# SyncE's issue order written out for the first two attention stages of a hybrid decoder block

## The chip, the cores and the metric

The kernel runs on one core of one Trainium2 chip. The core has five engines with a queue each: TensorE (PE) for matmuls, VectorE (DVE), ScalarE (ACT) and GpSimd (POOL) for everything else, and SyncE (SP), which in this kernel issues every DMA. An engine takes its instructions strictly in the order of its queue; an instruction that waits for a semaphore holds up all that stand behind it. A DMA's data is moved by 16 shared DMA engines after SP has issued it.

The metric is the time of one execution on the device, in microseconds (us). Before the change three runs took 628.25, 628.37 and 627.59 us; the median is 628.25 us.

## The reference: what is computed

One layer of a decoder block over 528 positions (16 learned meta tokens ahead of 512 tokens), width 1024, all in float32:

```
u    = RMSNorm(h)
proj = u @ w_in                # cq, ckv, k_pe, z_mla, fq, fk, fv, f_logit, z_fox, gate_a, gate_b
MLA:  q = RMSNorm(cq) @ w_uq   # 16 heads: 64 plain + 32 rotary columns
      k, v = RMSNorm(ckv) @ w_ukv;  k also has the shared rotary k_pe
      o_mla = causal softmax(q k^T / sqrt(96)) v
FoX:  cum = cumsum(log_sigmoid(f_logit + b))
      o_fox = causal softmax(fq fk^T / 8 + cum[t] - cum[s]) fv
y_mla = (o_mla * silu(z_mla)) @ w_br_mla;   y_fox = (o_fox * silu(z_fox)) @ w_br_fox
out   = h + RMSNorm((sig(gate_a) * y_mla + sig(gate_b) * y_fox) @ w_out)
```

## The kernel before

**Tiling.** Activations stay on the core, transposed, as a high and a low part (`uTh`, `uTl`). Each weight block of 128 columns is loaded by SP into one of three buffers `wraw` (line 133), cut by ACT into a high part `wh` (line 142) and by POOL, or DVE, into the rest `wl` (line 118), and multiplied in three passes. One such block with its matmuls and its ending is a `unit`; a unit's `make` cuts its weights and asks for the loads of the next three units (`nxt`).

**Stages.** Attention runs in 16 stages: for each of eight pairs of heads first the FoX branch (stages 0, 2, 4, ...), then the MLA branch (1, 3, 5, ...). A stage has, on PE, scores of the first three query blocks (`s0`), scores of the fourth (`s1`), and then the `fill`: the projections that the next stage needs. The values of a stage (`va`, tile `ov`) are computed in the stage after it, between that stage's `s0` and `s1`. Between scores and values lie the softmax (DVE takes the row bound `nb`; ACT the exponentials `sf`, line 693), the normalised probabilities `pn` in two float16 parts (ACT line 721, DVE line 722, meta columns by POOL lines 708 to 713), and their transposition into `pts` by DMA (line 729): for query blocks 0 to 3 two transfers each, of 3, 5, 7 and 9 tiles. `n0` issues the six of the first three blocks, `n1` the two of the fourth.

**Columns and rotary parts.** FoX scores add the cumulated gate by a fourth matmul with `CT`, whose two rows per head come from `c_dram` (line 280) when the pair's `fk` projection is done. MLA scores add the rotary part with `QP`, read from `qpe_dram` (line 507). The rotary projections are made in two halves (`pe_unit`): pairs 0 to 3 before stage 0, pairs 4 to 7 in stage 1's fill. Each half ends in `turn` (POOL, line 560), `rest` (ACT line 563, POOL line 118 on tile `gT`) and four writes of 256 KB to `qpe_dram` (line 566).

**Accumulators.** The projections of a fill share three PSUM accumulators (`acc`), the scores four banks (`stp`); a bank is free again when the engine that reads it is done.

**What sets the order.** PE's order is the written one in all of attention. In stage 0 POOL, ACT and DVE are in written order too. Everything else, SP's queue in all attention stages included, is placed by a scheduler that orders ready instructions by priorities and its own cost estimates.

In the trace's terms, `fq`, `fk`, `v`, `z`, `mq`, `mk` and `ppe` are units, `hlq` and `hlk` their results in two parts, `vT`, `vt`, `vm`, `vp` the steps of the values' operand, and `sil` the gated `z`.

Of the kernel before, what the change touches and what calls it, by code (L numbers as in the profile page):

```python
# [49 lines left out]
def f32(ap):  # L50
    return ap.bitcast(F32)
# [3 lines left out]
def block_kernel(ctx: ExitStack, tc: tile.TileContext, x, meta_tokens, pre_norm_g, w_in, fox_forget_b,  # L55
                 mla_q_norm_g, mla_kv_norm_g, w_uq, w_ukv, w_br_mla, w_br_fox, w_out, post_norm_g,
                 rope_tok, rope_pe, out):
    nc = tc.nc
# [32 lines left out]
    def mm(*a, **k):  # L91
        nc.tensor.matmul(*a, **k)  # L92
# [96 lines left out]
    def acc(name):  # L189
        return accp.tile([128, 512], F32, tag="acc", name=name)  # L190
# [3 lines left out]
    def unit(name, getw, act, nk, sls, done):  # L194

        st = {}
        out = []

        def make(*a):
            if "w" not in st:  # L200
                st["w"] = getw(*a)
                for load in getattr(out[0][1], "nxt", ()):
                    load()

        for i, sl in enumerate(sls):
            n = sl.stop - sl.start
            for k in range(nk):
                def fn(i=i, sl=sl, k=k, n=n):
                    make()
                    if k == 0:  # L210
                        st["ps"] = acc(f"{name}{i}")
                    ps = st["ps"][:, :n]
                    (wh, wl), (ah, al) = st["w"], act(k)
                    for q, (w, a) in enumerate(((wh, ah), (wh, al), (wl, ah))):
                        mm(ps, w(k), a[:, sl], start=(k == 0 and q == 0), stop=(k == nk - 1 and q == 2))
                    if k == nk - 1:
                        done(i, ps)
                out.append((3 * n / 2.4, fn))
        out[0][1].make = make
        if hasattr(getw, "load"):  # L220
            out[0][1].load = getw.load
        return out
# [16 lines left out]
    def run(steps):  # L239
        for _, fn in steps:  # L240
            fn()
# [227 lines left out]
    E_ = mybir.EngineType  # L469
    with ExitStack() as att:  # L470
# [35 lines left out]
        def load_qp(pr):  # L506
            nc.sync.dma_start(f32(QP), qpe_dram[2 * pr : 2 * pr + 2].rearrange("h i x f s -> (h i x f) s"))
# [123 lines left out]
        def z_unit(br, pr):  # L631
            def done(i, pz):
                sil = aw.tile([128, S], F32, tag="sil", name=f"sil{br}{pr}")
                with tc.high_priority(offset=60):
                    nc.scalar.activation(sil, pz, AF.Tanh, scale=0.5)
                    nc.vector.scalar_tensor_tensor(out=sil, in0=sil, scalar=1.0, in1=pz, op0=ALU.add, op1=ALU.mult)
                sils[br, pr] = sil
            return unit(f"z{br}{pr}", win_w((O_ZM, O_ZF)[br], pr), u_act, KD, REAL, done)

        def attention(br, pr):  # L640
# [4 lines left out]
            q, k = hls["q", br, pr], hls["k", br, pr]  # L645
# [11 lines left out]
            def sf_of(h, b):  # L657
                o, n = SF_STEP * (b % 3), 144 + 128 * b
                return sfs[b // 3][:, h, o : o + n]
# [38 lines left out]
            def norm(g):  # L698
                def fn(mid=int):
                    b0, nb_ = GRP[g][0], len(GRP[g])  # L700
                    su, ri = (sums[t][:, :, b0 : b0 + nb_] for t in ("su", "ri"))
                    nc.vector.tensor_scalar(out=su, in0=su, scalar1=1.0 / PSCALE, scalar2=None, op0=ALU.mult)
                    nc.vector.reciprocal(ri, su)  # L703

                    mt = aw.tile([128, 2, nb_, META], F32, tag=f"mt{g}", name=f"mt{nm_}{g}", bufs=1)
                    src = sfs[g][:, :, 0 : SF_STEP * nb_].rearrange("p h (b c) -> p h b c", b=nb_)[:, :, :, 0:META]
                    dst = pn[g][:, :, 0 : PN_STEP * nb_].rearrange("p h (b t) c -> p h b t c", b=nb_)[:, :, :, 0]
                    nc.gpsimd.tensor_tensor(out=mt, in0=src, in1=ri.unsqueeze(3).broadcast_to([128, 2, nb_, META]),  # L708
                                            op=ALU.mult)
                    hi, lo, hi2 = (dst[:, :, :, 32 * i : 32 * i + META] for i in range(3))  # L710
                    nc.gpsimd.tensor_copy(hi, mt)
                    nc.gpsimd.tensor_tensor(out=lo, in0=mt, in1=hi, op=ALU.subtract)
                    nc.gpsimd.tensor_copy(hi2, mt)
                    for b in GRP[g]:
                        for h in range(2):
                            sf = sf_of(h, b)[:, META:].rearrange("p (j c) -> p j c", c=128)
                            t0 = PN_STEP * (b % 3) + 1
                            hi, lo = (pn[g][:, h, t0 : t0 + 2 * b + 2].rearrange("p (j l) c -> p j l c", l=2)[:, :, i]
                                      for i in range(2))
                            rib = sums["ri"][:, h, b : b + 1]  # L720
                            nc.scalar.activation(hi, sf, AF.Copy, scale=rib)  # L721
                            nc.vector.scalar_tensor_tensor(out=lo, in0=sf, scalar=rib, in1=hi, op0=ALU.mult,  # L722
                                                           op1=ALU.subtract)
                    for b in GRP[g]:
                        if b == 1:
                            mid()
                        for h in range(2):
                            t0 = PN_STEP * (b % 3)
                            nc.sync.dma_start_transpose(
                                out=pts[h][:, 0 : 2 * b + 3, 128 * b : 128 * b + 128],  # L730
                                in_=pn[g][:, h, t0 : t0 + 2 * b + 3].rearrange("p t c -> p (t c)"))
                return fn
# [23 lines left out]
        def feed(br, pr):  # L756

            q = (q_mla, q_fox)[br](pr)
            k = (k_mla, k_fox)[br](pr)
            v, vts[br, pr] = v_unit(br, pr)  # L760
            return q, k, v
# [10 lines left out]
        for si, (br, pr) in enumerate(stages):  # L772
            last = si + 1 == len(stages)
            if not last:
                q, k, v = feed(*stages[si + 1])
            if br == 1:

                za, zb = z_unit(1, pr), z_unit(0, pr)
                fill = za + vts[br, pr] + q + zb[:4] + k + zb[4:6] + v + zb[6:]
            elif not last:  # L780
                fill = q[:3] + vts[br, pr] + q[3:] + k + v
            else:
# [5 lines left out]
                fill = g[:4] + vts[br, pr] + g[4:] + g2[:4] + [(100, g_scale)] + g2[4:]  # L788
            if si == 0:
                early = za[0][1], q[0][1], zb[0][1]  # L790
                rope0 = pe_turn, pe_rest
# [9 lines left out]
        late = []  # L801
        for si, (br, pr) in enumerate(stages):
            (s0, e0), (s1, e1), n0, n1, va = attention(br, pr)

            fill = fills[si]
            with ExitStack() as head:
                if si == 0:
                    head.enter_context(tc.manual_schedule(engines={E_.PE, E_.Pool, E_.Activation, E_.DVE}))
                    za, q, zb = early
                    turn, rest = rope0  # L810
                    za.make()
                    q.make()
                    lo = []
                    turn()
                    s0()
                    zb.make(nc.vector, lo)
                    e0({(0, 1): lambda: rest(1), (1, 1): lambda: rest(0)})
                    s1()
                    n0(lambda: load_qp(0))
                    lo[0]()  # L820
                    e1()
                    run(fill[:4])
                else:
                    s0()
                    e0()
                    for fn in late:
                        fn()
                    s1()
                    e1()
                    run(fill[:4])  # L830
                    n0()
            run(fill[4:11])
            n1()
            run(fill[11:])
            late = [va]
        run(tail[:4])
        mgates[0].make()
# [13 lines left out]
    with ExitStack() as mg:  # L851
# [42 lines left out]
        class Acts(Cuts):  # L894
            late = "BD"
# [26 lines left out]
        class Weights(Cuts):  # L922
            late = "BC"
# [4 lines left out]
            def load(self):  # L928
                p = self.p
                self.raw = raw = rwp.tile([128, 2, KD, 128], F32, tag="yraw", name=f"yraw{p}")  # L930
                for f in range(2):
                    c = 256 * p + 128 * f
                    nc.sync.dma_start(raw[:, f], wbr[1][:, :, c : c + 128])
                columns(self, f"1{p}")
                super().__init__(f"aop{p}", aop, 128, [raw[:, f] for f in range(2)], self.c[0])
# [69 lines left out]
        def make():  # L1005
            if todo:
                todo.pop(0).make()
            if todo:
                todo[0].load()
# [106 lines left out]
    with rctx, ExitStack() as og:  # L1116
# [29 lines left out]
        for c in range(4):  # L1146
            w = pre[c] if c < len(pre) else wout_unit(0, c)
# [68 lines left out]
```

## Time and profile before

| | |
|---|---|
| median of three runs | 628.25 us |
| profiled execution | 627.48 us, of which span from first to last instruction 625.1 us |
| mean granted TensorE clock | 0.992 |
| busy: PE, ACT, DVE, POOL | 601.1 (96%), 384.7, 380.8, 188.9 us |
| chain of waits, by engine | PE 92%, DVE 2%, ACT 2%, DMA 2%, SP's sequencer 1% |
| time that PE waited for transposed probabilities (`pt`) | 5.2 us, twice |

How to read it: a row of the timeline has the start in us from the span's start, the duration, the engine and line, the operation with its tiles and the count, and in brackets the idle time of that engine just before and what ended it. SPq is SP's sequencer; its rows are DMA issues, and a long one means that the issue itself took long. A row with a count covers several instructions of one kind. The granted clock is a share of full speed. All of attention lies between 71 and 414 us; stage 0 begins at 71.1, stage 1 at 89.97, stage 2 at 124.47 and stage 3 at 144.28 us.

### The profile page before, as it was taken

The numbers are of one execution on the slowest core, as the hardware profiler recorded it, in microseconds if no ns is written. First come the engines' busy times: TensorE is split into PE (matmuls) and PEld (weight loads), VectorE is DVE, ScalarE is ACT, GpSimd is POOL, SyncE is SP. The second block draws the span as 40 slices with busy tenths as digits, with TensorE's granted clock in tenths as the row PEclk, the third lists the DMA queues.
The fourth block names the chain that finished last, engine by engine and source line by source line (L and its number), as shares of the span: only waits on it lengthen the run. The fifth ranks groups of instructions, "written<-read, shape, count | busy, mean of one in ns | idle before, by whom it ended". The sixth has DMA issues, their size and how long they took to land.

```text
span 625.1 us, 11556 instructions
## 1 busy us (share of the span) xinstructions
PE 601.1 (96%) x4058; PEld 494.2 (79%) x4058; DVE 380.8 (61%) x1015; ACT 384.7 (62%) x838; POOL 188.9 (30%) x237
## 2 busy tenths in 40 slices
PE   3999997999999999999999999999999999999996
PEld 2879775988988989889889889887888875565885
DVE  3756566376477466565674773785977775655134
ACT  5746657388478477575774784786767754443421
POOL 3324632744425343353343444330000000003700
PEclk9999997999999999999999999999999999999998
DMA  8443577756647677557477467657253128333302
GB/s 280 130 84 91 102 164 171 187 139 152 167 109 168 164 130 149 140 138 182 102 166 180 103 159 150 159 140 201 73 157 97 46 70 266 104 102 101 102 34 102
DMA packets 204865, 85.40 MB, mean 137 GB/s; under 512 B 122684, under 2 KB 197820, under 8 KB 204808
## 3 DMA queue, kind: packets, MB, share of 16 engines
q1 hardware_dynamic: 204808, 84.67, 53.7%
q8 instruction: 32, 0.52, 0.3%
q14 instruction: 25, 0.20, 0.1%
HBM read 55.21 MB, written 4.26 MB: 95 GB/s over the span
## 4 chain that ended last, share of the span: by engine, by line
PE 92%; DVE 2%; ACT 2%; DMA 2%; SPq 1%; issue 0%; DVEq 0%; ACTq 0%
PE pg L92 14%; PE z L92 14%; PE v L92 8%; PE st L92 8%; PE fk L92 8%; PE po L92 7%; PE fq L92 7%; PE py L92 6%; PE ov L92 5%; PE yx L92 3%; PE psm L92 3%; PE mq L92 2%; PE yy L92 2%; PE vt L95 1%; PE mk L92 1%; DMA wsr<-in_w_in_dram 1%
## 5 line engine op out<-in xcount | busy, mean ns | idle before, releaser
L118 POOL TENSOR_TENSOR wl<-wraw,wh 128x1024 fp32r<-128x1024 f32 (+1 forms) x60 | 132.9, 2219 | 298.7 <-ACT wh L142 284.3
L142 ACT CAST wh<-wraw 128x1024 fp32r<-128x1024 f32 (+1 forms) x74 | 72.9, 986 | 88.0 <-issue 41.4
L693 ACT ACTIVATE sf<-sf,nb 128x144 f32<-128x144 f32 (+3 forms) x128 | 71.9, 565 | 6.1 <-DVE nb L683 6.1
L721 ACT ACTIVATE pn<-sf,ri 128x128 f16<-128x128 f32 (+3 forms) x128 | 61.9, 551 | 15.1 <-ACT sf L693 14.2
L722 DVE SCALAR_TENSOR_TENSOR pn<-sf,ri,pn 128x128 f16<-128x128 f32 (+3 forms) x128 | 65.7, 553 | 7.6 <-ACT pn L721 7.6
L92 PE MATMUL pg<-uTh,wh 128*128 128x512 f32 x128 | 51.9, 406 | 0.0
L92 PE MATMUL z<-uTh,wh 128*128 128x512 f32 x128 | 50.9, 398 | 0.0
L92 PE MATMUL z<-uTh,wl 128*128 128x512 f32 x128 | 50.1, 391 | 0.0
L92 PE MATMUL z<-uTl,wh 128*128 128x512 f32 x128 | 50.0, 391 | 0.0
L92 PE MATMUL pg<-uTh,wl 128*128 128x512 f32 x128 | 50.0, 391 | 0.0
L92 PE MATMUL pg<-uTl,wh 128*128 128x512 f32 x128 | 49.9, 390 | 0.0
L92 PE MATMUL st<-hlk,hlq 64*128 64x272 f32 (+3 forms) x480 | 48.3, 309 | 0.4 <-DVE nb L683 0.3
L683 DVE CUSTOM_DVE_ANT_0 sf<-st,maskt 128x272 f32<-128x272 f32 (+2 forms) x128 | 48.5, 435 | 0.1
L92 PE MATMUL py<-g,yw 128*128 128x512 f16 x192 | 42.6, 379 | 0.6 <-DVE yw L979 0.6
L92 PEld LDWEIGHTS st<-hlk,hlq 64*128 64x128 f32 x480 | 35.7, 187 | 6.8 <-ACT wh L142 2.5
L708 POOL TENSOR_TENSOR mt<-sf,ri 128x96 f32<-128x96 f32 (+1 forms) x32 | 9.5, 297 | 90.7 <-DVE ri L703 53.5
L92 PE MATMUL fk<-uTl,wh 128*128 128x256 f32 (+1 forms) x128 | 36.5, 285 | 0.0
L92 PE MATMUL v<-uTh,wh 128*128 128x256 f32 (+1 forms) x128 | 36.5, 285 | 0.0
L92 PE MATMUL fk<-uTh,wh 128*128 128x256 f32 (+1 forms) x128 | 36.5, 285 | 0.0
L92 PE MATMUL fk<-uTh,wl 128*128 128x256 f32 (+1 forms) x128 | 36.5, 285 | 0.0
L92 PE MATMUL v<-uTl,wh 128*128 128x256 f32 (+1 forms) x128 | 36.4, 285 | 0.0
L92 PE MATMUL v<-uTh,wl 128*128 128x256 f32 (+1 forms) x128 | 36.4, 284 | 0.0
(291 smaller groups left out, 1513.1 us busy)
## 6 DMA issues: line engine op xcount, KB each, us to landing
wraw<-in_w_in_dram SPq DMA_DIRECT2D x56, 512.0 KB, 4.5
yraw<-in_w_br_fox_dram SPq DMA_DIRECT2D x8, 512.0 KB, 6.1
yraw<-in_w_br_mla_dram SPq DMA_DIRECT2D x8, 512.0 KB, 3.6
wraw<-in_w_out_dram SPq DMA_DIRECT2D x8, 512.0 KB, 3.5
qpe_dram<-gT SPq DMA_DIRECT2D x8, 256.0 KB
pt<-pn SPq DMA_TRANSPOSE x128, 2.7
QP<-qpe_dram SPq DMA_DIRECT2D x8, 256.0 KB, 2.9
xr<-in_x_dram SPq DMA_DIRECT2D x4, 512.0 KB
```

The costliest lines, as they stand in the source:

```text
L92: nc.tensor.matmul(*a, **k)
L95: nc.tensor.transpose(*a)
L118: eng.tensor_tensor(out=lo, in0=src, in1=f32(hi), op=ALU.subtract)
L142: nc.scalar.copy(wh[:, :n], raw[:, :n])
L683: nc.vector.tensor_tensor_reduce(out=sf_of(h, b)[:, c0 : c0 + w], in0=ps[h][:, o : o + w], in1=maskt[:, m0 : m0 + w], scale=-scale, scalar ...
L693: nc.scalar.activation(sf, sf, AF.Exp, bias=sums["nb"][:, h, b : b + 1], scale=-1.0, accum_out=sums["su"][:, h, b : b + 1])
L708: nc.gpsimd.tensor_tensor(out=mt, in0=src, in1=ri.unsqueeze(3).broadcast_to([128, 2, nb_, META]), op=ALU.mult)
L721: nc.scalar.activation(hi, sf, AF.Copy, scale=rib)
L722: nc.vector.scalar_tensor_tensor(out=lo, in0=sf, scalar=rib, in1=hi, op0=ALU.mult, op1=ALU.subtract)
```

## The change

Three things are done.

1. In stages 0 and 1 SP is put in written order, as PE is.
2. In stage 0 the unit `zb` no longer asks for its next loads when its weights are cut: they go on the list `lo` and are issued behind `n1`, the last transpositions. In `n0` the load of `QP` moves from ahead of the second query block's transpositions to behind them.
3. In stage 1 the values of stage 0 are computed behind `s1` and not between `s0` and `s1`.

```
-        def make(*a):
+        def make(eng=None, later=None):
             if "w" not in st:
-                st["w"] = getw(*a)
-                for load in getattr(out[0][1], "nxt", ()):
-                    load()
+                st["w"] = getw(eng, later) if eng else getw()
+                loads = getattr(out[0][1], "nxt", ())
+                if later is None:
+                    for load in loads:
+                        load()
+                else:
+                    later.extend(loads)
...
                     for b in GRP[g]:
-                        if b == 1:
+                        if b == 2:
                             mid()
...
             with ExitStack() as head:
+                if si < 2:
+                    head.enter_context(tc.manual_schedule(engines={E_.PE, E_.SP}))
                 if si == 0:
-                    head.enter_context(tc.manual_schedule(engines={E_.PE, E_.Pool, E_.Activation, E_.DVE}))
...
+                    with tc.manual_schedule(engines={E_.PE, E_.SP, E_.Pool, E_.Activation, E_.DVE}):
...
                         zb.make(nc.vector, lo)
...
-                    lo[0]()
+                        lo.pop(0)()
...
                 else:
                     s0()
                     e0()
-                    for fn in late:
+                    for fn in late * (si > 1):
                         fn()
                     s1()
                     e1()
+                    for fn in late * (si == 1):
+                        fn()
                     run(fill[:4])
                     n0()
-            run(fill[4:11])
-            n1()
-            run(fill[11:])
+                run(fill[4:11])
+                n1()
+                if si == 0:
+                    for fn in lo:
+                        fn()
+                run(fill[11:])
             late = [va]
```

The diff does not show where the loads go. Three places do. The first is SP's queue from the rotary writes of stage 0 to the loads behind its transpositions. `wraw11` holds the weights of `fk` for pair 1, `wraw12` those of `v`, `wraw13` those of `z` (FoX), all for pair 1. Before:

```order
L566 DMA qpe_dram_80<-gT0_684 8x16x512 x4
L280 DMA CT_102<-c_dram_79 2x528
L729 DMA_TRANSPOSE pt0_661<-pn0_659 128x3x128
...
L507 DMA QP_651<-qpe_dram_80 128x512
L729 DMA_TRANSPOSE pt0_661<-pn0_659 128x5x128
...
L133 DMA wraw11_887<-in_w_in_dram 128x8x128
L729 DMA_TRANSPOSE pt1_662<-pn0_659 128x7x128
L133 DMA wraw12_1194<-in_w_in_dram 128x8x128
L729 DMA_TRANSPOSE pt0_661<-pn1_660 128x9x128
L729 DMA_TRANSPOSE pt1_662<-pn1_660 128x9x128
L133 DMA wraw13_1265<-in_w_in_dram 128x8x128
```

And now:

```order
L570 DMA qpe_dram_80<-gT0_684 8x16x512 x4
L733 DMA_TRANSPOSE pt0_661<-pn0_659 128x3x128
...
L733 DMA_TRANSPOSE pt1_662<-pn0_659 128x5x128
L511 DMA QP_651<-qpe_dram_80 128x512
L733 DMA_TRANSPOSE pt0_661<-pn0_659 128x7x128
...
L733 DMA_TRANSPOSE pt1_662<-pn1_660 128x9x128
L133 DMA wraw11_1021<-in_w_in_dram 128x8x128
L133 DMA wraw12_1199<-in_w_in_dram 128x8x128
L511 DMA QP_651<-qpe_dram_80 128x512
```

The two columns of `CT` for pair 1 and the loads 11 to 13 no longer stand among stage 0's transpositions.

The second place is the same queue from stage 1's transpositions to the loads for stage 2: there `CT`, `wraw13`, `wraw14` (`mq` of pair 1) and `wraw15` (`z` of MLA, pair 1) have gone. Before:

```order
L729 DMA_TRANSPOSE pt1_662<-pn0_659 128x7x128
L729 DMA_TRANSPOSE pt0_661<-pn1_660 128x9x128
L729 DMA_TRANSPOSE pt1_662<-pn1_660 128x9x128
L133 DMA wraw15_1378<-in_w_in_dram 128x8x128
L133 DMA wraw16_1544<-in_w_in_dram 128x8x128
L566 DMA qpe_dram_80<-gT0_684 8x16x512 x4
L133 DMA wraw17_1615<-in_w_in_dram 128x8x128
```

And now:

```order
L733 DMA_TRANSPOSE pt1_662<-pn0_659 128x7x128
L133 DMA wraw13_1270<-in_w_in_dram 128x8x128
L733 DMA_TRANSPOSE pt0_661<-pn1_660 128x9x128
L733 DMA_TRANSPOSE pt1_662<-pn1_660 128x9x128
L570 DMA qpe_dram_80<-gT0_684 8x16x512 x4
L133 DMA wraw14_1317<-in_w_uq_dram 128x2x64 x2
L133 DMA wraw14_1317<-in_w_ukv_dram 128x2x64 x2
L284 DMA CT_102<-c_dram_79 2x528 x2
L133 DMA wraw15_1383<-in_w_in_dram 128x8x128
L133 DMA wraw16_1550<-in_w_in_dram 128x8x128
```

`wraw13` stands behind six of stage 1's eight transpositions, and `CT`, which stage 2's scores read, behind the second half's rotary writes and `wraw14`.

The third place is ACT's queue where stage 1's exponentials begin. Before:

```order
L142 CAST wh10_1261<-wraw10_839 128x512
L142 CAST wh11_1308<-wraw11_887 128x1024
L635 ACTIVATE sil00_1078<-z000_1021 128x512
L605 ACTIVATE vT00_1069<-v000_1053,vsc00_1057 128x272
L605 ACTIVATE vT00_1069<-v001_1059,vsc00_1057 128x256
L693 ACTIVATE sf000_1084,su00_1082<-sf000_1084,nb00_1081 128x144
```

And now:

```order
L142 CAST wh10_1266<-wraw10_841 128x512
L609 ACTIVATE vT00_1071<-v000_1055,vsc00_1059 128x272
L639 ACTIVATE sil00_1080<-z000_1023 128x512
L609 ACTIVATE vT00_1071<-v001_1061,vsc00_1059 128x256
L142 CAST wh11_1313<-wraw11_1021 128x1024
L697 ACTIVATE sf000_1089,su00_1087<-sf000_1089,nb00_1086 128x144
```

The cast of `wraw11` now stands behind `sil` and `vT`, but still ahead of the first exponential. On every engine the set of instructions is the same as before.

More of the change, by code (lines that the diff above doesn't have):

```diff
@@ L806, in block_kernel @@
             with ExitStack() as head:
+                if si < 2:
+                    head.enter_context(tc.manual_schedule(engines={E_.PE, E_.SP}))
                 if si == 0:
-                    head.enter_context(tc.manual_schedule(engines={E_.PE, E_.Pool, E_.Activation, E_.DVE}))
[L809 to L819, printed above, removed]
-                    lo[0]()
-                    e1()
-                    run(fill[:4])
+                    with tc.manual_schedule(engines={E_.PE, E_.SP, E_.Pool, E_.Activation, E_.DVE}):
+                        za, q, zb = early
+                        turn, rest = rope0
+                        za.make()
+                        q.make()
+                        lo = []
+                        turn()
+                        s0()
+                        zb.make(nc.vector, lo)
+                        e0({(0, 1): lambda: rest(1), (1, 1): lambda: rest(0)})
+                        s1()
+                        n0(lambda: load_qp(0))
+                        lo.pop(0)()
+                        e1()
+                        run(fill[:4])
                 else:
```

## The prediction

> **What bounds the kernel now.** I read the page's chain of waits first: PE holds 92% of it, so a change is worth what it does to PE's queue. The second view is what PE waits for over the span; the one row of any size that lies in attention is this (us in total, times, longest):
>
> ```profile
> PE ov L92 <- DMA pt<-pn: 5.2, 2, 4.8
> ```
>
> The third is the chain in order of time, once at stage 1 and once at stage 3, an undisturbed MLA stage (start, us, what):
>
> ```profile
> 91.83 2.67 SPq L729
> 94.60 3.41 DMA pt<-pn
> 98.15 3.81 PE ov L92 x22
> 101.95 1.85 PE st L92 x17
> 103.81 2.28 PE fq L92 x9
> ...
> 144.35 2.29 PE st L92 x29
> 146.64 1.97 PE ov L92 x26
> 148.60 1.42 PE st L92 x14
> 150.02 2.28 PE fq L92 x9
> ```
>
> In stage 3 scores, values and scores take 150.02 - 144.35 = 5.67 us. In stage 1 the same work runs from 89.97 to 103.81, 13.84 us; the first and the last row of its first scores, from the timeline:
>
> ```profile
> 89.97 0.56 PE L92 MATMUL st<-hlk,hlq 64*128 64x144 f32 x6
> ...
> 91.98 0.35 PE L92 MATMUL st<-KPL,QP 64*128 64x400 f32 x2
> ```
>
> The excess, 8.2 us, is 5.2 us of waiting for stage 0's last transposition and 3.0 us of slowness afterwards. The slowness is in the clock, by the fourth view (window, us, PE busy and count, PEld, DVE, ACT, POOL, granted clock, DMA share, GB/s):
>
> ```profile
> 95.00:96.00 1.00, 0.00 (x0) 0.00 (x0) 0.72 (x2) 0.99 (x3) 1.00 (x1) 1.00 1.22 308
> 96.00:97.00 1.00, 0.00 (x0) 0.00 (x0) 1.00 (x7) 0.78 (x3) 1.00 (x1) 0.53 1.28 287
> 101.00:102.00 1.00, 1.00 (x13) 0.79 (x8) 0.01 (x1) 1.00 (x3) 0.17 (x1) 0.50 0.08 15
> 103.00:104.00 1.00, 1.00 (x15) 0.86 (x12) 0.90 (x5) 0.00 (x0) 0.00 (x0) 1.00 0.00 0
> ```
>
> PE has been idle since 92.3; the clock halves at about 96 and is back by 103. So **8.2 us is the most that the change can win** here.
>
> **Part 1: stage 0's transpositions get ahead of the loads.** SP's queue before:
>
> ```profile
> 78.94 2.86 SPq L729 DMA_TRANSPOSE pt<-pn  x1
> ...
> 84.84 0.36 SPq L507 DMA_DIRECT2D QP<-qpe_dram  x1
> 85.27 3.88 SPq L729 DMA_TRANSPOSE pt<-pn  x3
> 89.26 0.52 SPq L133 DMA_DIRECT2D wraw<-in_w_in_dram  x1
> 96.05 0.53 SPq L133 DMA_DIRECT2D wraw<-in_w_in_dram  x1
> ```
>
> One transposition costs SP 3.88 / 3 = 1.29 us when it need not wait. The first starts at 78.94 in both orders (it waits for POOL's part of `pn`) and ends at 81.80. Behind it seven at 1.29 and `QP` at 0.45 end at 81.80 + 9.03 + 0.45 = 91.3, where the chain before has its last issue from 94.60 to 95.95. Landing 3.41 after its start, the last is there at 93.4 in place of 98.0. PE meanwhile has `s1` ahead of the values. Its banks come free once DVE has read `s0`, which is 2.2 us of DVE work that can begin at about 91.7, since `sil` no longer stands behind a weight cast on ACT; so `s1` ends near 95.2, the values near 97.2, and `fq` begins there and not at 103.81. **This wins 6.6 us, for the moment.** `QP` lands some 2.9 us after 85.8, before its use at 90.4.
>
> **Part 2: what has been put behind them.** Three loads are late now.
>
> ```profile
> 93.70 1.04 ACT L142 CAST wh<-wraw 128x1024 fp32r<-128x1024 f32 x1 [4.51 <-DMA wraw<-in_w_in_dram]
> 96.22 0.42 ACT L693 ACTIVATE sf<-sf,nb 128x144 f32<-128x144 f32 x1 [0.24 <-DVE nb L683]
> 112.71 1.05 ACT L142 CAST wh<-wraw 128x1024 fp32r<-128x1024 f32 x1 [1.26 <-issue]
> ...
> 126.61 0.41 ACT L693 ACTIVATE sf<-sf,nb 128x144 f32<-128x144 f32 x1
> 131.64 1.22 SPq L729 DMA_TRANSPOSE pt<-pn  x1
> ```
>
> `wraw11` (weights of `fk`) was issued at 89.26 and cast at 93.70, 4.4 us later. It is now issued at 91.4, so it is cast from 95.8 to 96.9. That cast stands ahead of stage 1's exponentials, which start at 96.9 and not 96.22: ACT has gained nothing from PE's lead. From the first exponential to the first transposition is 131.64 - 126.61 = 5.03 us in stage 2; so stage 1's first one goes at 101.9, and six of them hold SP until 109.7.
>
> PE does not keep its 6.6 us either. `fk` needs an accumulator, and the first to come free is that of `fq`, read by a cast that ACT reaches only after eight exponentials and eight `pn` pieces (page, mean ns of one):
>
> ```profile
> L693 ACT ACTIVATE sf<-sf,nb 128x144 f32<-128x144 f32 (+3 forms) x128 | 71.9, 565 | 6.1 <-DVE nb L683 6.1
> L721 ACT ACTIVATE pn<-sf,ri 128x128 f16<-128x128 f32 (+3 forms) x128 | 61.9, 551 | 15.1 <-ACT sf L693 14.2
> ```
>
> That is 8 x 0.565 + 8 x 0.551 = 8.9 us, and with the casts of `vp`, `vm`, `wraw12` and `fq` itself (2.7 us) 11.6 us from 96.9: 108.5, with DVE's part some 109.4. PE, which needs 9.0 us for the rest of `fq` and `ppe` (103.81 to 112.8 before), is through with them at 106.2 and waits 3.2 us.
>
> `wraw13` (weights of the next FoX `z`) was issued at 96.05. Now it stands behind six transpositions: issue 109.7, there 4.4 us later at 114.1, cast to 115.2. Before, that cast ended at 113.76. It is not `z` that suffers, but what stands behind `wl13` on POOL:
>
> ```profile
> 113.84 2.40 POOL L118 TENSOR_TENSOR wl<-wraw,wh 128x1024 fp32r<-128x1024 f32 x1 [0.38 <-ACT wh L142]
> 116.20 2.55 POOL L560 TENSOR_TENSOR gT<-gT 128x512 f32<-128x512 f32 x2
> 118.71 2.54 POOL L118 TENSOR_TENSOR gT<-gT,gT 128x512 fp32r<-128x512 f32 x2
> 118.18 3.78 SPq L566 DMA_DIRECT2D qpe_dram<-gT  x4
> 119.73 0.44 DVE L118 TENSOR_TENSOR hlk<-fk,hlk 128x272 fp32r<-128x272 f32 x1 [5.16 <-ACT hlk L266]
> 124.87 0.27 PE L92 MATMUL st<-CT,ONE 64*128 64x144 f32 x2
> ```
>
> Everything from `wl13` on moves with it by 1.4 us: `turn`, the `gT` casts, the rotary writes (to 121.96 before, now to 123.3), and behind the `gT` casts on ACT `hlk`, whose second part on DVE frees the accumulator for the last half of `v`: 120.2 before, 121.5 now. So PE's lead is used up before stage 2 begins: `v` ends at 124.4, as before.
>
> Then comes **the columns `CT`**, which before were loaded in stage 0, hidden by 40 us of other work. Stage 2's scores read them from the fourth matmul on, at 124.87. Now four small loads and `CT` follow the rotary writes:
>
> ```profile
> 97.20 0.88 SPq L133 DMA_DIRECT2D wraw<-in_w_uq_dram  x2
> 98.13 0.97 SPq L133 DMA_DIRECT2D wraw<-in_w_ukv_dram  x2
> 74.19 3.51 SPq L566 DMA_DIRECT2D qpe_dram<-gT  x4
> pt<-pn SPq DMA_TRANSPOSE x1, 5.9
> wraw<-in_w_in_dram SPq DMA_DIRECT2D x1, 512.0 KB, 7.5
> DMA to landing us min/median/max: 2.0/2.0/2.0
> ```
>
> (The last three rows are times from issue to landing: of the transposition at 78.94, of a weight load issued at 122.5 behind the second rotary writes, and of `CT` in general.) SP reaches `CT` at 123.3 + 0.05 + 1.9 = 125.3 and ends its two issues at 126. How long they take to land behind 1 MB of writes, no row shows; the bounds are these. Below, the 2.0 us of a free queue: 127.8. Above, what was issued behind rotary writes: the transposition of 78.94 landed at 84.8, which is 84.8 - 77.1 = 7.7 us after the fourth write was issued (77.70 less 0.6), the weight load at 130.0, 8.6 us after it (121.4). With the fourth write at 122.7 that gives 130.4 to 131.3. I take **130.0**, near the two rows that stand behind the same writes, less something because `CT` is only 4 KB. PE then loses 130.0 - 124.9 = **5.1 us** (2.9 to 6.4) against before.
>
> [...]
>
> **Part 3: the clock.** PE is idle from 124.6 to 130.0, 5.4 us, as long as the gap of 5.2 us before, which cost 13.84 - 5.67 - 5.2 = 3.0 us of slow matmuls. I take 3.0 again, with 0 as the lower bound, because the gaps of 3.2 us stay under the 4 us after which the clock fell. [...]
>
> **Part 4: behind it.** `wraw15` follows `CT` and its cast stands ahead of stage 2's exponentials, so these start 8 to 10 us later than 126.61. Stage 2's transpositions land later by as much, and PE needs them later by 8.1. The slack before is small, since the values of stage 2 follow at 146.64. I count 0, with up to 1.5 us as the upper bound. From stage 4 on the queues are as before, and PE is the bound, so nothing is won back.
>
> **Sum.** 5.1 + 3.0 + 0 = 8.1 us over the profiled execution's 627.48, so 635.6. That execution lies 0.8 us below the median of 628.25; with half of this added I forecast **636.0 us**, 1.2% slower. Its own range goes from 2.9 + 0 to 6.4 + 3.0 + 1.5: 630.8 to 639.2.
>
> **The rivals.**
>
> *The lateness cancels, no change.* If `CT` lands within 2.0 us and `wraw13` is early enough, or if `CT` alone does not matter, stage 2 is still held by `hlk` and the last half of `v`, which end at 124.4 as before: 628.0. Likewise with `wraw13` early and `CT` late: ACT then casts it at 108.5, the whole chain comes 5.5 us earlier, and `CT` lands at 124.5. For: stages elsewhere absorb such shifts. Against: two late loads in one chain. 10%.
>
> *Faster.* Both at once: `wraw13` early and `CT` landing 2.0 us after its issue, at 120.5 + 2.0 = 122.5; then 2.4 us of the lead survive, 625.9 us. With all the lead kept it would be 628.25 - 8.2 = 620.0. The point from which it decides is `CT` landing before 124.3. For: the gap of 5.2 us goes for certain. Against: the rows of 5.9 and 7.5 us, and six transpositions ahead of `wraw13`. 10%.
>
> *Slower by more.* ACT held by `wraw15` makes PE wait for stage 2's transpositions as well: up to 3 us more, 639 us. It lies in the forecast's 80%, as a fifth of it.
>
> A measurement of this kernel tells apart about 0.2%, 1.3 us. From these cases: faster 10%, same 10%, slower 80%. The range that should hold the time 8 times in 10 is **628.0 to 639.5**: it leaves out the faster case, half of the no-change case and a few per cent above.
>
> **What would show it.** Right: in the waits, no `ov` row on `pt` in stage 1, and a new row for `st` on the DMA of `CT` of 4 to 6 us; the first exponential of stage 1 at about 97; the weight load before stage 1's last two transpositions at about 110; the second rotary writes past 122; the granted clock at half for some us after 128. Wrong: no wait of PE at the start of stage 2, or stage 2 beginning before 123; then the chain over POOL was not the bound. If PE waits there for `hlk` and not for `CT`, the place is right and the term is not.

## The result: 1.5% slower, and where the time stands in the profile after

| | before | after |
|---|---|---|
| median | 628.31 us (4 runs beside it) | 637.83 us (637.26 to 638.64, 4 runs) |
| ratio, 95% interval | | 1.0153 [1.0136, 1.0171] |
| span of the profiled execution | 625.1 us | 635.3 us |
| mean granted clock | 0.992 | 0.988 |
| `fq` of stage 1 begins | 103.81 us | 97.55 us |
| stage 2's first matmul with `CT` | 124.87 us | 132.59 us |
| stage 3 begins | 144.35 us | 154.97 us |

The change does what it says in stage 1 and loses more in stage 2. Stage 3 begins 10.6 us later, which covers the span's 10.2 us. The row of 5.2 us for `ov` on `pt` is gone; in its place PE waits in stages 1 and 2 for three other things (us in total, times, longest):

```profile
PE st L92 <- DMA CT<-c_dram: 3.6, 1, 3.6
PE fk L92 <- DVE hlq L118: 3.5, 1, 3.5
PE v L92 <- DVE hlk L118: 3.2, 1, 3.2
```

The chain of waits of the changed kernel, in order of time, over the same stretch as the one shown of the kernel before:

```profile
95.50 2.05 PE ov L92 x25
97.55 2.27 PE fq L92 x9
...
130.13 2.42 DMA CT<-c_dram
132.59 3.00 PE st L92 x18
135.59 3.61 PE ov L92 x26
139.19 1.17 PE st L92 x16
140.36 5.67 PE z L92 x24
...
154.97 2.29 PE st L92 x30
```

The lead of 6.3 us on `fq` is there, and it is gone before stage 2. SP's queue (its rows are issues) shows what is late:

```profile
93.36 1.20 SPq L133 DMA_DIRECT2D wraw<-in_w_in_dram  x2
...
103.17 7.80 SPq L733 DMA_TRANSPOSE pt<-pn  x6
111.02 0.58 SPq L133 DMA_DIRECT2D wraw<-in_w_in_dram  x1
...
121.94 3.72 SPq L570 DMA_DIRECT2D qpe_dram<-gT  x4
125.71 3.35 SPq L133 DMA_DIRECT2D wraw<-in_w_uq_dram  x2
129.10 0.98 SPq L133 DMA_DIRECT2D wraw<-in_w_ukv_dram  x2
130.13 0.62 SPq L284 DMA_DIRECT2D CT<-c_dram  x2
```

and ACT's casts of `wraw11`, `wraw13`, `wraw14` and `wraw15`, each with the time that ACT stood idle for the load:

```profile
97.09 1.05 ACT L142 CAST wh<-wraw 128x1024 fp32r<-128x1024 f32 x1 [5.02 <-DMA wraw<-in_w_in_dram]
...
116.51 1.05 ACT L142 CAST wh<-wraw 128x1024 fp32r<-128x1024 f32 x1 [7.21 <-DMA wraw<-in_w_in_dram]
...
133.59 0.62 ACT L142 CAST wh<-wraw 128x512 fp32r<-128x512 f32 x1 [9.90 <-DMA wraw<-in_w_ukv_dram]
135.09 1.04 ACT L142 CAST wh<-wraw 128x1024 fp32r<-128x1024 f32 x1 [0.88 <-DMA wraw<-in_w_in_dram]
```

All four loads are late, and so is `CT`. At the start of stage 2 the profile names `CT` alone as what PE waited for. Whether the others count too, only runs can tell.

### The profile page after: what moved, and what is told of

Its sections match the earlier page's. It is cut to its first block, busy times and chain, and to the rows that moved or that the text cites. A ratio compares the mean times of both kernels' runs of the same rounds, so it can differ in the third digit from the quotient of the medians.

```text
span 635.3 us, 11541 instructions
## 1 busy us (share of the span) xinstructions
PE 606.3 (95%) x4058; PEld 498.3 (78%) x4058; DVE 381.6 (60%) x1015; ACT 384.1 (60%) x838; POOL 188.8 (30%) x237
## 4 chain that ended last, share of the span: by engine, by line
PE 89%; DVE 3%; DMA 2%; SPq 2%; ACT 2%; POOL 1%; issue 0%; DVEq 0%; ACTq 0%
PE pg L92 14%; PE z L92 14%; PE st L92 8%; PE v L92 7%; PE po L92 7%; PE fq L92 7%; PE fk L92 6%; PE py L92 6%; PE ov L92 5%; PE yx L92 3%; PE psm L92 3%; PE mq L92 2%; PE yy L92 2%; PE vt L95 1%; PE mk L92 1%; DMA wsr<-in_w_in_dram 1%
## 5 line engine op out<-in xcount | busy, mean ns | idle before, releaser
L92 PE MATMUL st<-hlk,hlq 64*128 64x272 f32 (+3 forms) x480 | 49.9, 312 | 0.7 <-DVE nb L687 0.5
L92 PEld LDWEIGHTS <-yw 128*128 128x128 f16 x192 | 17.8, 98 | 22.7 <-DVE yw L990 1.1
```

## The experiments

The changed kernel delays three groups of transfers in stages 0 to 2: **C**, the columns `CT`; **Z**, `wraw13`, the weights of `z`; **M**, `wraw14` and `wraw15`, the weights of `mq` and of MLA's `z`. Six kernels bring them forward again, alone and together, with all else as in the changed kernel; four others ask what its parts do. Each was compared with the kernel before in the same session (its median was 628.31 beside the changed kernel, 627.89, 626.96 and 627.71 us in the three others), so the table gives the difference from that:

| brought forward | median, us | against before, us | ratio, 95% interval |
|---|---|---|---|
| nothing (the changed kernel) | 637.83 | +9.5 | 1.0153 [1.0136, 1.0171] |
| C | 637.55 | +9.7 | 1.0151 [1.0133, 1.0168] |
| Z | 632.80 | +4.9 | 1.0071 [1.0047, 1.0095] |
| M | 634.92 | +8.0 | 1.0123 [1.0101, 1.0146] |
| C and Z | 631.69 | +3.8 | 1.0062 [1.0042, 1.0082] |
| C and M | 628.85 | +1.9 | 1.0024 [1.0006, 1.0042] |
| C, Z and M | 626.06 | -0.9 | 0.9983 [0.9968, 0.9998] |

### C: the columns early

```
# k_fox, done:
-            if pr and i:
+            if pr > 1 and i:
# stage 0, behind n1 and the loads of lo:
+                    for h in range(2):
+                        nc.sync.dma_start(f32(CT[64 * h : 64 * h + 2, :]), c_dram[:, 2 + h, :])
```

> The changed kernel, but the two columns of CT for pair 1 are loaded in stage 0, behind its last transpositions (one weight load ahead of them). Theory (CT behind the rotary writes holds PE at the start of stage 2): the fourth matmul of stage 2's scores no longer waits, stage 2's scores run on at 128.4 us from the span's start, where v ends, and most of the slow clock behind the wait goes too; 7 us off 637.8, so 630 to 632. The wait of 3.2 us of v for hlk stays. Rival A (ACT, held by the late weights of mq, is the next bound, so that PE waits for stage 3's transpositions instead): 634 to 635, with an ov row on pt. Rival B (the late weight load wraw13 alone is the cause): no change, 637 to 638.

Measured: 637.55 us, no change. The wait for `CT` is gone and the loss is not. The wait of `v` for `hlk` is still there, with 3.7 us, and in stage 2 PE waits for others; these two rows of the waits are new:

```profile
PE vt L95 <- DVE nb L687: 2.8, 1, 2.8
PE mk L92 <- DVE sil L640: 2.2, 1, 2.2
```

Both hang on ACT, whose exponentials of stage 2 begin behind the casts of `wraw14` and `wraw15`:

```profile
133.31 0.62 ACT L142 CAST wh<-wraw 128x512 fp32r<-128x512 f32 x1 [9.72 <-DMA wraw<-in_w_ukv_dram]
135.21 1.05 ACT L142 CAST wh<-wraw 128x1024 fp32r<-128x1024 f32 x1 [1.28 <-DMA wraw<-in_w_in_dram]
136.90 0.41 ACT L697 ACTIVATE sf<-sf,nb 128x144 f32<-128x144 f32 x1
```

That is where they began in the changed kernel (136.78), and 10.3 us later than before the change (126.61). So my theory of the cause fell. Rival A had the right engine, but looked for the wait at the next stage's transpositions and expected it to cost less than `CT` did. The wait that the profile names was one of two ways through stage 2 that came out equally late; taking it away lets the other show.

### Z: `wraw13` early

```
# stage 0, behind n1 and the loads of lo (the first unit of stage 2's fill is z of FoX):
+                    fills[2][0][1].load()
```

> The changed kernel, but the load wraw13 (z of FoX, pair 1) is issued in stage 0, behind its last transpositions, and not behind six of stage 1's. CT stays behind the rotary writes. Theory (two late loads in one chain): ACT casts it at 109.3 and not at 116.5, wl13 ends at 113.7, the rotary writes end at about 119.4 and not 125.7, so CT lands at about 126.8 and not 132.6; v no longer waits for hlk and ends at about 125. PE waits for CT only about 1 us: 629 to 630. Rival B (wraw13 alone): the same 628 to 629, told apart by the next run. Rival C (wraw13 is not in the chain): CT stays at 132 and the time at 637 to 638.

Measured: 632.80 us. The chain over POOL moved the expected way: the cast comes at 111.57, 4.9 us earlier than in the changed kernel though 2.3 us later than expected, the wait of `v` is gone, and PE waits for `CT` by

```profile
PE st L92 <- DMA CT<-c_dram: 1.7, 1, 1.7
```

But the time stands 3 us above the expected 629 to 630. The casts of `wraw14` and `wraw15` again stand ahead of stage 2's exponentials, which begin at 133.06 us.

### C and Z

> The changed kernel with both loads early: wraw13 and the two columns of CT behind stage 0's last transpositions. Theory: no wait of PE at the start of stage 2, which begins near 125, since the lead of 6.3 us on fq is used up by the wait of 3.5 us for hlq and the slow clock behind it; 627.5 to 629, the same as the kernel before. Rival (the lead is kept once both loads are early): 622 to 624. Rival B (only wraw13 matters): equal to the run with wraw13 alone.

Measured: 631.69 us, above both. Stage 2 begins at 124.01 us, as the theory has it, and stage 3 only at 150.33, since the exponentials begin at 131.06. Beside Z alone that is 1.1 us less, which lies within the scatter of the two runs (630.24 to 634.22 and 630.79 to 633.21 us); that the rest of the loss is M's, the run with all three shows (below).

### M: the weights of `mq` and `z` early, alone and with C

```
# where stage 2's fill is made (its first units: z of FoX, mq, z of MLA):
+            if si == 2:
+                early2 = za[0][1], q[0][1], zb[0][1]
...
# stage 1, ahead of n1 and behind it:
+                if si == 1:
+                    early2[1].load()
                 n1()
+                if si == 1:
+                    early2[2].load()
```

> The changed kernel, but the weights of the two units that stage 2 needs behind its scores (mq and z of MLA, pair 1: wraw14 and wraw15) are loaded ahead of the rotary writes and not behind them; CT stays behind the writes, wraw13 behind six transpositions. Theory (two ways lead through stage 2 side by side, one of PE over CT, one of ACT and DVE over these weights, and the later one counts): alone it gives back little. CT follows the writes directly, its issue takes the stall of about 2 us that the mq weights had, it lands near 131, stage 3 begins 1.5 us earlier: 635 to 637. Rival (ACT's way alone is the bound, CT costs nothing): 631 to 632.

> The changed kernel with CT early and wraw14 and wraw15 early; wraw13 stays behind six transpositions. Theory (two ways side by side): each alone gives almost nothing, both together take stage 2's lateness away but for the wait of v for hlk; stage 2's scores begin at 128.4 us, stage 3 at 148 to 149.5 and not at 155: 631 to 632.5. Rival (the loss adds up from independent terms, of which CT is 0): as with wraw14 and wraw15 early alone.

Measured: 634.92 us alone, and 628.85 with C. This is the test of the two ways. By the differences in the table C alone gains nothing, M alone 1.5 us, and both together 7.6. That loss did not add up from terms: it was the later of two ways through stage 2, one of PE over `CT` and one of ACT and DVE over `wraw14` and `wraw15`. The first exponential of stage 2 shows it as well. With C alone it waits for the casts (136.90 us, above). With M alone the casts are done in time and it waits for the scores, and they for `CT`:

```profile
132.71 0.42 ACT L697 ACTIVATE sf<-sf,nb 128x144 f32<-128x144 f32 x1 [5.21 <-DVE nb L687]
```

With both it begins at 126.88, as before the change (126.61). With C and M stage 3 begins at 144.60 us, earlier than I had expected, because `wraw13` landed sooner as well (last section), which M's 1.5 us may owe a part to too; the profiled execution, at 626.89 us, is also the fastest of its ten.

The run with M alone also bears on what sets `CT`'s landing. It is issued right behind the writes there, with the four small loads out of the way. The last write's issue, `CT`, and what waits for it in the chain:

```profile
123.31 0.93 SPq L570
124.29 6.39 DMA CT<-c_dram
130.73 3.00 PE st L92 x18
```

In the changed kernel the same three are

```profile
125.08 0.58 SPq L570
...
130.13 2.42 DMA CT<-c_dram
132.59 3.00 PE st L92 x18
```

`CT` is issued 1.0 us behind the last write in the one and 5.0 us behind it in the other. It lands 7.4 us (130.68 - 123.31) and 7.5 us (132.55 - 125.08) after that write was issued in both. So it looks as if the writes decide, and not the place behind them. The first run says so by itself: 6.39 us from issue to landing, against the 2.0 us that loads of 2.1 KB (`CT<-ch`, ahead of attention) took in the kernel before. In the changed kernel `CT`'s own 2.42 us does not say it, since there the issue was late: the four small loads ahead of it held SP for 4.4 us. But the first of these loads, issued 0.6 us behind the last write, took 7.1 us from issue to landing and came in at 132.8, beside `CT`:

```profile
wraw<-in_w_uq_dram SPq DMA_DIRECT2D x2, 64.0 KB, 7.1
```

(The row covers two loads; the time is that of the first.) The figure is not quite a constant: the first matmul with `CT` begins 7.4 and 7.5 us after the last write's issue in these two kernels, and 7.0 us after it with `wraw13` early (121.09 and 128.07). How the writes delay it, no run shows.

### C, Z and M, and the scheduler's own queue in stage 1

> The changed kernel with all of them early: CT and wraw13 behind stage 0's transpositions, wraw14 ahead of stage 1's last two, wraw15 behind them, all ahead of the rotary writes; SP in written order in both stages. Theory: stage 2 begins at 124 to 125, stage 3 at 144 to 145.5, 627 to 628.5, the time of the kernel before, since PE still waits 3.5 us for hlq and runs slowly behind it. Rival (written order itself costs, by what stands between): above 630.

```
# the changed kernel, SP in written order in stage 0 alone:
-                if si < 2:
+                if si < 1:
                     head.enter_context(tc.manual_schedule(engines={E_.PE, E_.SP}))
```

> The changed kernel, but SP is in written order in stage 0 alone; in stage 1 the scheduler places its queue again, which puts CT among stage 0's transpositions and wraw13 and wraw14 ahead of stage 1's. The values stay behind both score groups. Theory (the loss is all in stage 1's written order of SP): as with both loads early, 627.5 to 629.5; stage 0's written order and the later values gain nothing lasting, since PE waits 3.5 us for hlq. Rival (the later values, or stage 0's late wraw11, cost something by themselves): above 631.

Measured: 626.06 us with all three brought forward by hand, 0.17% below the kernel before, and 627.71 us with the scheduler's queue in stage 1 (ratio 0.9999 [0.9985, 1.0012]), which puts `CT`, `wraw13` and `wraw14` early as well, and `wraw15` ahead of the rotary writes. So the whole loss was in the place of these transfers behind stage 0. Written order cost nothing by itself. What the two do not have is the 6 us: in both, PE waits for `hlq`, 3.4 and 2.6 us, and then runs slowly. With all three early the chain reads

```profile
110.89 7.66 PE fk L92 x48
118.55 5.84 PE v L92 x48
124.39 1.88 PE st L92 x24
```

The same 48 matmuls of `fk` took 5.84 us before the change. Stage 2 begins where it did before.

### The third part taken out, and alone

```
# the changed kernel, the values of stage 0 between the score groups again:
-                    for fn in late * (si > 1):
+                    for fn in late:
                         fn()
                     s1()
                     e1()
-                    for fn in late * (si == 1):
-                        fn()
```

> The changed kernel without its third part: in stage 1 the values of stage 0 stand between the two score groups again. Theory (PE's lead is used up by the wait of 3.5 us for hlq, which hangs on ACT's late exponentials and not on PE): PE waits some 2 us for stage 0's last transposition, fq begins 1 to 1.5 us later, at 98.5 to 99, and the wait for hlq shrinks by as much: 637 to 638.5, as the changed kernel. Rival (the place of the values counts by itself): 639 to 640.5.

The kernel before with the reverse of this edit:

> The kernel before with the third part alone: SP's queue stays with the scheduler in both stages, and in stage 1 the values of stage 0 stand behind both score groups. Theory: PE does the second score group while it waits for stage 0's last transposition (there at 98.0), so fq begins at 101 and not at 103.8; ACT's exponentials of the fourth block, which wait 2.7 us for DVE in the kernel before, come as much earlier, so hlq and fk do too, and no load is late: 1.5 to 2.8 us faster than the kernel before. Rival (the lead is absorbed, as in the changed kernel, by a wait for hlq): within 0.6 us of the kernel before.

Measured: 637.38 us without the third part (ratio to before 1.0150 [1.0131, 1.0170], as the changed kernel), and 628.28 us with it alone (1.0005 [0.9992, 1.0018]). It counts for nothing in either. In the first, `fq` begins at 97.60 us, sooner than I had expected, and then PE waits for DVE's row bound of the fourth block as long as it waited for `hlq`:

```profile
103.60 0.66 PE L95 MATMUL vt<-ident,vT 128*128 128x128 f32 x4 [3.65 <-DVE nb L687]
```

In the second, my expectation missed by 2 us. PE never gets to do `s1` during its wait, because the score banks are not free:

```profile
96.36 1.64 PE L92 MATMUL st<-hlk,hlq 64*128 64x272 f32 x6 [4.01 <-DVE nb L683]
```

DVE reads the banks in order behind `sil`, and `sil` waits on ACT behind the cast of `wraw11`:

```profile
95.03 0.69 DVE L636 SCALAR_TENSOR_TENSOR sil<-sil,z 128x512 f32<-128x512 f32 x1 [5.06 <-ACT sil L635]
```

So the wait of 5.2 us for `pt` had a second wait of nearly the same length lying under it. It takes the late `wraw11`, which puts its cast behind `sil`, for the third part to work at all. The reverse does not hold: `fq` begins at 97.60 us without the third part and at 97.55 with it, so the order of SP in stage 0 brings the lead by itself. Whether the third part is worth anything where the lead is kept, no run shows.

### Keeping the lead: stage 1's exponentials ahead of the late cast

The last question is where the lead of 6 us goes once no load is late. By the chain, it goes to `hlq`, which ACT reaches behind its exponentials, which stand behind the cast of `wraw11`. This kernel has all three groups early, and in stage 1 ACT's order is written out:

```
+                        if si == 1:
+                            mid.enter_context(tc.manual_schedule(engines={E_.PE, E_.SP, E_.Activation}))
+                            early_q.make()     # fq
+                            early_pe.make()    # ppe
                         s0()
                         e0()
...
                         s1()
                         e1()
+                        if si == 1:
+                            early_k.make()     # fk: the cast of wraw11
```

> As the run before, and ACT in written order over the exponentials of stage 1, with the casts of fq and ppe ahead of them and the cast of wraw11 (fk) behind them. Theory (the lead of 6 us on fq is lost because that cast, waiting for a load issued behind the transpositions, stands ahead of stage 1's exponentials, and with them all that precedes the cast hlq): the first exponential at 93 and not at 98, hlq at about 105, PE's wait for it gone, fk from 107 and not from 110; 4 to 5 us off the run before: 622 to 624.5, faster than both kernels. Rival (the lead is lost later anyway, or the cast is late for fk): 627 to 628.5.

Measured: 623.61 us (622.64 to 623.95), ratio 0.9937 [0.9917, 0.9956]: faster than both kernels. Against the run before, 626.06 us, it gains 2.45 us, where I had expected 4 to 5. The first exponential and `fk`:

```profile
93.56 0.42 ACT L697 ACTIVATE sf<-sf,nb 128x144 f32<-128x144 f32 x1 [0.61 <-DVE nb L687]
...
109.58 0.39 PE L92 MATMUL fk<-uTh,wh 128*128 128x272 f32 x1 [1.77 <-DVE hlq L118]
```

Stage 2 begins at 121.53 us, 3.0 us earlier than before the change. That `fk` is not at 107 as expected has a cause on DVE: ACT's part of `hlq` is done at 106.4, but on DVE a `pn` piece of 2.26 us (106.67) stands ahead of the second part. About 1.8 us are left there.

## Why the prediction was right, point by point

The forecast was 636.0 us, with 628.0 to 639.5 as the range; measured are 637.83. It had the sign and the size. Its account of the cause holds only half, and part of the size is luck, as the points show. One slip in the sum: the bounds 630.8 and 639.2 stand on different bases, 627.9 and 628.25; on the first they are 630.8 and 638.8.

- **The limit of 8.2 us and part 1.** Right. No `ov` row on `pt` is left; `fq` begins 6.3 us earlier, where I had 6.6. Stage 0's last transposition was issued by 93.3 and not 91.3, but as `s1` ends at 95.5 this did not matter.
- **Part 2, the first exponential.** 98.04 for 96.9, `hlq` done on DVE at 110.0 for 109.4, the wait of `fk` 3.5 us for 3.2. Right, and the run with the exponentials first shows that the cast of `wraw11` is what held them.
- **Part 2, `wraw13`.** Issued at 111.02 for 109.7, cast at 116.51 for 114.1. The delay of everything behind it was 2.4 us larger than my 1.4: 1.3 us from the issue and 1.1 us from a landing of 5.4 us where I had 4.4. All the rest of the chain follows: the fourth rotary write at 125.08 for 122.7, and `v`, which waited 3.2 us for `hlk`. It did not end at 124.4, as I had it; stage 2's first scores begin only at 128.37.
- **The term for `CT`.** This is the one that was mis-sized: 5.1 us forecast; against before `CT`'s matmul came 7.7 us later. 0.7 us of that was there already at 26 us, in a part of the kernel that has not changed, so 7.0. It lies above my upper bound of 6.4. The step from the writes to the landing was right in sum (130.0 less 122.7 is 7.3, measured 7.5), but not in its parts: I had `CT`'s issue 2.6 us behind the fourth write and its landing 4.7 us after that, and measured are 5.0 and 2.4 us. What the term is short of, 1.9 us, are the 2.4 us of `wraw13`, less the 0.7 us that was there already, and 0.2 us of the landing.
- **Part 3, the clock.** From `CT` to `z` 7.77 us pass, where it was 4.69: 3.1 us, for 3.0. The figure was right and its reasons were not. The 3.0 was carried over from a gap of 5.2 us because PE was to be idle for 5.4; it was idle for 3.55, since `v` ended so late, and by my own 4 us, taken from the one gap in the kernel before (PE idle from 92.3, the clock down at about 96), that gap should have cost nothing. This is luck. The reason for giving the other gaps nothing was wrong too. Behind the gap of 3.5 us ahead of `fk` the clock did go to half (us, PE busy and count, PEld, DVE, ACT, POOL, granted clock, DMA share, GB/s):

```profile
108.00:109.00 1.00, 0.00 (x0) 0.00 (x0) 0.93 (x3) 1.00 (x2) 0.10 (x1) 1.00 0.72 164
...
112.00:113.00 1.00, 1.00 (x6) 1.00 (x6) 0.42 (x1) 0.00 (x0) 0.00 (x0) 0.50 0.65 125
114.00:115.00 1.00, 1.00 (x6) 1.00 (x6) 0.00 (x0) 0.00 (x0) 0.00 (x0) 0.51 2.05 257
115.00:116.00 1.00, 1.00 (x10) 1.00 (x10) 0.00 (x0) 0.00 (x0) 0.00 (x0) 1.00 0.60 22
```

  The slow stretch cost 1.7 us (the 48 matmuls of `fk` take 7.49 and not 5.84 us) and did not show in the time only because `v` then waited for `hlk` anyway. Behind the gap of 3.2 us ahead of `v` it was at half again, from 125.2 to 128.6 us, and PE then waited for `CT`.
- **Part 4, counted at 0.** As a term added to that of `CT` the 0 held: behind `CT` PE waits for nothing more in stage 2 of the changed kernel. What failed is that the way over ACT was given no price of its own. "PE needs them later by 8.1" holds only as long as `CT` holds PE as well. With `CT` early alone the loss stays, at 9.7 us, so the lateness of `wraw14` and `wraw15` was worth as much as that of `CT`; with these two early and `CT` late it is still 8.0. The sum came out because the two lie side by side and one was counted. Whoever had acted on it and moved `CT` alone would have gained nothing.
- **The rivals.** "`wraw13` early and `CT` late: 628.0" was measured at 632.8, and "both early: 625.9" at 631.7. Both left out the way over ACT, and the first had `CT` land at 124.5, where it was 128.0. With that way freed too, the time was 0.9 us below the kernel before, where the second had 2.4.

Not tried: Z and M together with `CT` late, the landing of `CT` with no writes ahead of it at the changed kernel's own time, the fastest kernel without the third part, and `hlq` ahead of the last `pn` on DVE.

## What to carry to other kernels

A wait in the profile is the last of those that end together. Before a gain or a loss is put down to it, look at what else was delayed past the same point, and take each away alone and both together: if one alone gives nothing and both give nearly everything, they lie side by side. When a queue is put in written order, list every transfer that the scheduler had placed early, small ones too, and follow each to its reader; here 8 KB of columns and two weights behind 1 MB of writes, and a third weight behind six transpositions, turned a lead of 6 us into a loss of 9.5. And a lead on one engine is kept only if the engine that frees its next buffer gets the same lead.

## What the runs showed of the hardware

**In one run half clock followed a gap of 1.7 us, in others none came behind gaps of 1.7 to 2.8 us; where it came, it began up to 1.5 us after PE had started again.** With the scheduler's queue in stage 1 it followed a gap of 2.6 us; the row of the gap, and the clock in the windows behind it:

```profile
111.74 0.39 PE L92 MATMUL fk<-uTh,wh 128*128 128x272 f32 x1 [2.61 <-DVE hlq L118]
```

```profile
112.00:113.00 1.00, 1.00 (x10) 1.00 (x10) 1.00 (x3) 0.00 (x0) 1.00 (x2) 1.00 0.58 130
113.00:114.00 1.00, 1.00 (x6) 1.00 (x6) 1.00 (x2) 0.00 (x0) 1.00 (x1) 0.51 0.58 129
...
116.00:117.00 1.00, 1.00 (x9) 1.00 (x8) 0.00 (x0) 0.48 (x1) 1.00 (x2) 0.78 0.11 14
```

The clock went to half at 113.0 us, 1.3 us after PE was back, until about 116.4; the 48 matmuls of `fk` took 7.65 us there. In the fastest kernel a gap of 1.8 us at the same place left it at 1.00 in every window from 106 to 126 us. But the length of the gap alone did not decide. With `wraw13` early, a gap of 1.7 us was followed by half clock as well:

```profile
128.07 0.50 PE L92 MATMUL st<-CT,ONE 64*128 64x144 f32 x2 [1.71 <-DMA CT<-c_dram]
```

```profile
129.00:130.00 1.00, 1.00 (x10) 0.66 (x7) 0.84 (x7) 0.15 (x1) 0.00 (x0) 0.66 0.97 276
130.00:131.00 1.00, 1.00 (x7) 0.39 (x8) 1.00 (x7) 0.46 (x1) 0.46 (x1) 0.50 1.08 307
```

With the scheduler's queue in stage 1 the clock was also at half from 96.0 to 99.4 us, beside two gaps of 0.6 and 0.7 us (ahead of `ov`, until 95.62 and 96.72). With C and M a gap of 1.7 us (ahead of `v`, until 121.68) left it at 1.00, and behind one of 2.8 us with C alone (ahead of `vt`, until 141.94) the matmuls of `z` followed each other at 0.23 us, as ahead of it. Each is one execution. In the windows from 92 to 142 us, eleven of the twelve traces have such stretches (the fastest kernel's has none). Each lasts 3.4 or 6.8 us, and where a trace has more than one, each ends 10.2 to 20.5 us behind the one before, within 0.05 us a whole number of times 3.41 us. In the changed kernel the clock is at half from 111.58 to 114.99, from 125.23 to 128.64 and from 132.06 to 138.88 us (by the means of the windows: 0.79 from 111 to 112 puts the first drop at 111.58). What decides whether the clock falls behind a gap stays open.

**The load of `wraw13` took 3.75 to 5.88 us to land, and the cause is open.** It took 5.39 us to land where a transposition followed 0.76 us after its issue (111.78), and 3.75 us where four small loads stood between and the transposition followed 2.9 us after it (113.78). Without the third part it took 4.38 us, though the transposition followed 0.68 us after it (112.57):

```profile
111.02 5.39 DMA wraw<-in_w_in_dram
```

```profile
110.87 3.75 DMA wraw<-in_w_in_dram
```

```profile
111.89 4.38 DMA wraw<-in_w_in_dram
```

The rows are those of the changed kernel, of the run with M alone and of the run without the third part. The first is the 1.1 us by which I had the landing too short. A transposition close behind may slow the load: the run with C has 5.88 us with one 0.74 us behind. But the third row speaks against its being the whole cause, and it was not tested by itself.
